# adaLN tiles of a hybrid decoder step in groups, from buffers of their own

## The chip, the cores and the metric

The kernel runs on one core of a Trainium2 chip. The metric is the device time of one execution in microseconds (us): the median of three runs. One further execution was recorded by the profiler; all rows below are from that one. The engines are named as in the profile: PE is TensorE (PEld its weight loads), DVE is VectorE, ACT is ScalarE, POOL is GpSimd, and SP is SyncE, whose queue issues nearly all loads.

## The reference

One step of a decoder trunk of two layers, over 320 token columns: 256 of a prompt and 8 x 8 of eight sample sequences. Layer 0 mixes tokens with a gated MLP over chunks, layer 1 with a Mamba-2 scan; each is followed by an MLP with a squared ReLU. Every sub-layer is preceded by an RMS norm whose shift, scale and gate come from a conditioning vector c for each of nine sequences (adaLN).

```
mod = (silu(c) @ ada_w[i] + ada_b[i]).reshape(c.shape[0], N_MOD, D_MODEL)   # 9 x 6 x 1024, for i in 0, 1
h = modulate(rms_norm(x, norm1_g[i]), mod[:, 0], mod[:, 1])                 # h * (1 + scale) + shift
z = gelu(h @ w_in); u = z[..., :2048]; v = layer_norm(z[..., 2048:], ln_g, ln_b)
y = (u * s) @ w_out            # s: v mixed along the tokens by w_s, plus b_s
x = x + mod[:, 2] * y
x = x + mod[:, 5] * (square(relu(modulate(...) @ w1)) @ w2)
```

The matrix ada_w is read whole, 1024 x 6144 floats for each layer, and multiplies only nine rows.

## The kernel before

**Weights.** All weights are float32 and come in tiles of 128 x 1024 (512 KB). raw_tile takes one of NRAW = 6 slots; split (lines 131 to 136) makes of a tile a rounded part whi (ScalarE, L134) and the rest wlo (VectorE, L135), in NHI = 3 pairs of buffers. A product is three matmuls, hi x hi, lo x hi and hi x lo (mm3: L299 to L301 in the profile). A slot is free again when wlo is made.

**adaLN.** A tile of ada_w is not split. TensorE multiplies it with sc, the silu of c (32 columns), as four instructions of 128 x 256, each into 32 partitions of one PSUM bank (L157). A unit (l, f), f being one of the six parts of layer l, takes eight tiles; then ScalarE copies the sums (L168), four short matmuls turn them (L171) and VectorE adds the bias (L174). Ten units go through ada_unit, a generator that stops after each tile. They are a filler: wload, the loader of weights, takes one step of it for each weight tile (RATE0 = 1.0; RATE1 = 0.7 in the first MLP). need(l, f) runs it until a unit is done. Parts (0, 0) and (0, 1), shift and scale of the first norm, don't go this way.

**First stage.** For kt in 0 to 7 two tiles of ada0 (shift and scale of the 128 features kt) are loaded, multiplied (L429), copied by ScalarE (L439), turned by four short matmuls (L442) and added (L445, L446). With them the features kt of x are normalised into hhi and hlo (L257 to L259; L448 to L455 for the sample columns, also into hs), and a tile of gm_wv0 (the first half of v's weights) is loaded and split. Then 16 matmuls over 512 columns (v_mm: L403 to L407) add these features' part to the first half of v. The loads for kt + 1 are written before the matmuls of kt.

**Second stage.** The second half of v (gm_wv, wload), with adaLN steps between. Then vx, the sample rows, is put together with a copy vs (L471, L472), the layer norm of v runs on VectorE in two halves q (L508 with the row lng, L509 with lnb; these are broadcast loads, one buffer each, in the pool gp that stays open), and 16 projections u (gm_wu) follow, with the mixing matmuls (spatial) from the tenth on. Then come w_out, MLP, the Mamba stage (w_in; there bc and ea, rows spread over all partitions, are loaded through the same queue, L632 and L633), its w_out, and the second MLP.

**Order.** A scheduler orders the instructions by a timeline of its own and places each engine's instructions in a row. Every engine works its row in order; so does SyncE, where a load that waits for a buffer holds all loads behind it. hs and vs lie in a pool g1 that is closed before the norm; a second pool g1, for bsr, wsT and bd, takes its place.

## Time and profile before

| | |
|---|---|
| three runs | 1102.05, 1106.19, 1108.08 us; median 1106.19 |
| the profiled execution | 1104.12 us, its span 1102.3 us |
| TensorE, matmuls | busy 1055.1 us (96%), 7809 records |
| VectorE, ScalarE, POOL | 658.6, 547.1, 315.9 us |
| adaLN of the ten units (L157) | 640 records, 52.9 us busy, mean 390 ns |
| loads by SP's queue | 200.47 MB, 55.5% of the DMA engines' time |

How to read it: TensorE's matmuls overlap, and their ends are modelled, so a busy share says little; the distance from one start to the next is what a matmul costs. One float32 matmul instruction makes two records: a tile of adaLN, four instructions, is a row of "x8". A row of the timeline joins equal instructions that follow each other; in square brackets stands the idle time before it, and what ended it. A row of the busy time by windows has, behind the window and its length, the busy us and (in brackets) the count of PE, PEld, DVE, ACT and POOL, then the granted clock of TensorE as a share of full speed, the DMA share and GB/s.

### The profile page before, as it was taken

Reading aid. Unit: us, or ns where it says so; the run is one execution under the profiler, and the core shown is the slowest. Engines: PE = TensorE matmul, PEld = TensorE weight load, DVE = VectorE, ACT = ScalarE, POOL = GpSimd, SP = SyncE. Lnnn points to the kernel's source line nnn. Section 1 sums busy time; section 2 is a strip of 40 time slices with the busy share of each in tenths; the row PEclk is TensorE's granted clock in tenths of the full one; section 3 lists DMA queues with packets and bytes.
Section 4 is the critical chain, followed back from the end, with each engine's and each line's share of the span. In section 5 each row is a group of like instructions: output and inputs, shape, how many; then the busy total and the mean of one; then the engine's idle time right before and its main releaser. Section 6 shows DMA issues by size and latency. Waiting matters only on the chain.

```text
span 1102.3 us, 19778 instructions
## 1 busy us (share of the span) xinstructions
PE 1055.1 (96%) x7809; PEld 971.5 (88%) x7809; DVE 658.6 (60%) x1080; ACT 547.1 (50%) x1013; POOL 315.9 (29%) x403
## 2 busy tenths in 40 slices
PE   5999999999999999999997989999899999999996
PEld 3677899889899889999996879999899899999996
DVE  3544956445744433445995898988866764443342
ACT  4443333434544433334879666787435455543331
POOL 1200124332333312113361343434325243320111
PEclk9999999999999999999998998999999999999998
DMA  8877885675777767545444555655445565444531
GB/s 330 305 234 231 282 316 186 213 245 177 239 216 219 220 219 222 169 145 194 131 149 152 204 199 191 207 200 203 144 140 183 180 216 167 153 147 143 152 95 48
DMA packets 60877, 213.97 MB, mean 194 GB/s; under 512 B 6560, under 2 KB 12128, under 8 KB 58480
## 3 DMA queue, kind: packets, MB, share of 16 engines
q1 hardware_dynamic: 58544, 200.47, 55.5%
q0 software_dynamic: 1952, 11.98, 3.1%
q8 instruction: 61, 1.00, 0.4%
q14 instruction: 32, 0.26, 0.1%
q10 hardware_dynamic: 288, 0.26, 0.1%
HBM read 199.31 MB, written 12.85 MB: 192 GB/s over the span
## 4 chain that ended last, share of the span: by engine, by line
PE 71%; ACT 8%; DVE 6%; issue 5%; DMA 4%; POOL 3%; POOLq 0%; ACTq 0%; SPq 0%; DVEq 0%
PE mm L299 19%; PE mm L301 18%; PE mm L300 18%; PE adap L157 4%; ACT bc L646 2%; ACT whi L134 2%; DVE wlo L135 2%; DVE co L608 1%; DMA bc<-rowd 1%; PE ax L716 1%; PE mm L403 1%; PE mm L404 1%; PE mm L405 1%; POOL Y L728 1%; PE ax L299 1%
## 5 line engine op out<-in xcount | busy, mean ns | idle before, releaser
L135 DVE TENSOR_TENSOR wlo<-raw,whi 128x1024 fp32r<-128x1024 f32 (+1 forms) x243 | 297.2, 1224 | 225.1 <-ACT whi L134 224.1
L134 ACT ACTIVATE whi<-raw 128x1024 fp32r<-128x1024 f32 (+1 forms) x243 | 254.8, 1050 | 277.2 <-PE mm L300 197.9
L299 PE MATMUL mm<-hhi,whi 128*128 128x320 f32 x952 | 305.4, 321 | 11.1 <-ACT cb L601 5.3
L300 PE MATMUL mm<-hlo,whi 128*128 128x320 f32 x952 | 298.8, 314 | 0.9 <-DVE hlo L831 0.8
L301 PE MATMUL mm<-hhi,wlo 128*128 128x320 f32 x952 | 298.4, 314 | 0.0
L299 PEld LDWEIGHTS mm<-hhi,whi 128*128 128x128 f32 x952 | 182.0, 191 | 29.0 <-issue 13.0
L300 PEld LDWEIGHTS mm<-hlo,whi 128*128 128x128 f32 x952 | 182.5, 192 | 2.0 <-DVE hlo L831 1.1
L301 PEld LDWEIGHTS mm<-hhi,wlo 128*128 128x128 f32 x952 | 182.0, 191 | 0.7 <-issue 0.2
L299 PE MATMUL mm<-mhi,whi 128*128 128x320 f32 x512 | 159.1, 311 | 0.0
L301 PE MATMUL mm<-mhi,wlo 128*128 128x320 f32 x512 | 158.1, 309 | 0.0
L300 PE MATMUL mm<-mlo,whi 128*128 128x320 f32 x512 | 157.9, 308 | 0.0
L350 POOL TENSOR_TENSOR ta<-ta 128x320 f32<-128x320 f32 x64 | 81.5, 1275 | 142.3 <-ACT ta L348 126.8
L299 PEld LDWEIGHTS mm<-mhi,whi 128*128 128x128 f32 x512 | 96.1, 188 | 4.1 <-issue 4.1
L300 PEld LDWEIGHTS mm<-mlo,whi 128*128 128x128 f32 x512 | 96.1, 188 | 0.0
L301 PEld LDWEIGHTS mm<-mhi,wlo 128*128 128x128 f32 x512 | 96.1, 188 | 0.0
L285 POOL TENSOR_TENSOR x<-x,rs 128x64 f32<-128x64 f32 x28 | 12.1, 431 | 222.8 <-DVE rs L284 222.8
L351 ACT ACTIVATE mhi<-ta 128x320 fp32r<-128x320 f32 x64 | 30.1, 470 | 79.1 <-POOL ta L350 79.1
L352 DVE TENSOR_TENSOR mlo<-ta,mhi 128x320 fp32r<-128x320 f32 x64 | 34.7, 548 | 53.7 <-ACT mhi L351 53.7
L608 DVE SCALAR_TENSOR_TENSOR co<-cb,vec,co 128x344 f32<-128x344 f32 x96 | 54.5, 580 | 7.4 <-ACT co L606 7.2
L157 PE MATMUL adap<-raw,sc 128*32 128x256 f32 x640 | 52.9, 390 | 0.2 <-DMA raw<-ada_w 0.2
L602 POOL COPY cvp<-cb 128x3 f32<-128x3 f32 x32 | 24.1, 753 | 70.3 <-ACT cb L600 70.2
L282 DVE SCALAR_TENSOR_TENSOR x<-mm,mod,x 128x256 f32<-128x256 f32 x29 | 14.0, 483 | 46.5 <-PE mm L301 45.2
(340 smaller groups left out, 1752.0 us busy)
## 6 DMA issues: line engine op xcount, KB each, us to landing
raw<-mlp_w SPq DMA_DIRECT2D x128, 512.0 KB, 3.9
raw<-ada_w SPq DMA_DIRECT2D x80, 512.0 KB, 4.4
raw<-w_in SPq DMA_DIRECT2D x48, 512.0 KB, 3.6
raw<-ada SPq DMA_DIRECT2D x16, 512.0 KB, 5.9
raw<-gm_wv SPq DMA_DIRECT2D x16, 512.0 KB, 5.5
raw<-gm_wu SPq DMA_DIRECT2D x16, 512.0 KB, 5.5
raw<-gm_wo SPq DMA_DIRECT2D x16, 512.0 KB, 4.5
st<-state SPq DMA_DIRECT2D x8, 1024.0 KB, 5.5
```

What stands on the lines that cost most here:

```text
L134: act.activation(hi[:, :n], raw[:, :n], AF.Copy)
L135: eng.tensor_tensor(lo[:, :n], raw[:, :n], hi[:, :n].bitcast(F32), SUB)
L157: pe.matmul(ps[32 * j : 32 * j + 32, :256], lhsT=sc[:, k, :], rhs=r[:, j * 256 : (j + 1) * 256], start=(k == 0), stop=(k == KD - 1), skip_ ...
L299: pe.matmul(ps[:, :n], lhsT=whi[:, kk, :], rhs=hi, start=first, stop=False)
L300: pe.matmul(ps[:, :n], lhsT=whi[:, kk, :], rhs=lo, start=False, stop=False)
L301: pe.matmul(ps[:, :n], lhsT=wlo[:, kk, :], rhs=hi, start=False, stop=last)
L350: pool.tensor_tensor(s, t, t, MUL)
L351: act.activation(mhi[:, m, :], s, AF.Copy)
L352: dve.tensor_tensor(mlo[:, m, :], s, mhi[:, m, :].bitcast(F32), SUB)
L602: pool.tensor_copy(cvp[:, ct, :], cb[:, TP : TP + 3])
L608: dve.scalar_tensor_tensor(o[:, :CO], cb[:, k : k + CO], wv(k), o[:, :CO], MUL, ADD)
L646: act.activation(bc[:, h, cq[c]], bc[:, h, cq[c]], AF.Relu, bias=nat[:, c, HG * g_ + h : HG * g_ + h + 1], scale=-1.0)
```

## The change

**First stage.** ada0 and gm_wv0 come from a pool of ten slots of their own (raw0), closed after the stage. The loads go in groups of kt, (0), (1, 2), (3, 4), (5, 6), (7): first the adaLN tiles of a group, then its v tiles. The adaLN products of a group are written together, the last-loaded tile first, ahead of the v matmuls of the group before; each half of the PSUM bank takes one kt.

**Later adaLN tiles.** ada_unit loads four tiles into buffers of their own (ara, AB = 4), one a step, and after the fourth writes all 16 instructions at once, the last-loaded tile first. The number of steps for a unit stays eight.

**Room.** NRAW goes from 6 to 5; lng and lnb go into the second pool g1; the ring of descriptors for POOL's transfers gets 4096 bytes.

**Second stage.** Its instructions are not to be scheduled before the first stage's last load (issue_after).

```diff
-NRAW = 6
+NRAW = 5
+AB = 4
+NRAW0 = 10
...
     def ada_unit(l, f):
         ps = ada_ps()
-        for k in range(KD):
-            r = raw_tile()
-            nc.sync.dma_start(r, io["ada_w"][l, k * P : (k + 1) * P, f * 1024 : (f + 1) * 1024])
-            for j in range(4):
-                pe.matmul(
...
-            if k < KD - 1:
+        for kb in range(0, KD, AB):
+            rs = []
+            for k in range(kb, kb + AB):
+                r = wp.tile([P, 8 * P], F32, tag="ara", name=nm("ara"), bufs=AB)
+                nc.sync.dma_start(r, io["ada_w"][l, k * P : (k + 1) * P, f * 1024 : (f + 1) * 1024])
+                rs.append(r)
+                if len(rs) < AB:
+                    yield True
+            for i in (AB - 1, *range(AB - 1)):
+                for j in range(4):
+                    pe.matmul(
...
+            if kb + AB < KD:
                 yield True
...
+    s0, s0p = new_pool("right")
     def load(src):
-        raw = raw_tile()
-        nc.sync.dma_start(raw, src)
+        raw = s0p.tile([P, 8 * P], F32, tag="raw0", name=nm("raw0"), bufs=NRAW0)
+        aw["last"] = nc.sync.dma_start(raw, src).ins
...
+    kgs = [(0,), (1, 2), (3, 4), (5, 6), (7,)]
+    def ada_load(kg):
+        for kt in kg:
+            aw[kt] = [load(io["ada0"][kt, hf]) for hf in range(2)]
+        for kt in kg:
+            vw[kt] = load(io["gm_wv0"][kt])
+
+    def ada_mm(kg):
+        ps = ada_ps()
+        for kt, hf in [(kt, hf) for kt in reversed(kg) for hf in (1, 0)]:
+            o = 256 * (kt - kg[0])
+            for j in range(4):
+                pe.matmul(
+                    ps[32 * j : 32 * j + 32, o : o + 256],
...
+        for kt in kg:
+            o = 256 * (kt - kg[0])
+            sb = scratch()
+            act.copy(sb[:, :256], ps[:, o : o + 256])
...
+    for kg in kgs[:2]:
+        ada_load(kg)
+    ada_mm(kgs[0])
+    ada_mod(0)
+    ki = 1
+    for kt in range(KD):
+        if kt % 2 == 0 and ki < len(kgs):
+            ada_mm(kgs[ki])
+            ki += 1
+            if ki < len(kgs):
+                ada_load(kgs[ki])
+        elif kt % 2:
+            for k in kgs[ki - 1]:
+                ada_mod(k)
+        whi, wlo = split(vw[kt])
...
+    with tc.issue_after(aw["last"]):
+        for j in range(2, 4):
...
-        gg = gp.tile([P, 1024], F32, tag="lng", name=nm("lng"))
-        be = gp.tile([P, 1024], F32, tag="lnb", name=nm("lnb"))
+        gg = g1.tile([P, 1024], F32, tag="lng", name=nm("lng"))
+        be = g1.tile([P, 1024], F32, tag="lnb", name=nm("lnb"))
...
-    nc = bacc.Bacc("TRN2", target_bir_lowering=False, num_devices=1)
+    nc = bacc.Bacc("TRN2", target_bir_lowering=False, num_devices=1, dynamic_dma_scratch_size=4096)
```

The places in the new order on which the steps rest follow. A number in a name tells one buffer's fill from the next; whi and wlo carry that of their split, and the lines are each kernel's own.

TensorE at the start, before: raw_177 to raw_184 are the adaLN tiles of kt 0 and 1, and L403 is the first v matmul.

```order
L429 MATMUL adap_181<-raw_177,sc 32x256 x4
L202 MATMUL nrm_143<-ones_d,acc_141 128x1 x3
L429 MATMUL adap_181<-raw_179,sc 32x256 x4
L197 MATMUL nrm_154<-nid,nx_147 128x128 x2
L197 MATMUL nrm_154<-nid,nx_147 128x64
L442 MATMUL adap_181<-cst,ta_200 128x10 x2
L429 MATMUL adap_235<-raw_182,sc 32x256 x4
L429 MATMUL adap_235<-raw_184,sc 32x256 x4
L403 MATMUL mm_171<-whi_196,hhi 128x512
```

After, the same place:

```order
L210 MATMUL nrm_143<-ones_d,acc_141 128x1 x3
L446 MATMUL adap_198<-raw_182,sc 32x256 x4
L446 MATMUL adap_198<-raw_180,sc 32x256 x4
L205 MATMUL nrm_154<-nid,nx_147 128x128 x2
L205 MATMUL nrm_154<-nid,nx_147 128x64
L463 MATMUL adap_198<-cst,ta_207 128x10 x2
L446 MATMUL adap_213<-raw_192,sc 32x256 x4
L446 MATMUL adap_213<-raw_190,sc 32x256 x4
L446 MATMUL adap_213<-raw_188,sc 32x256 x4
L446 MATMUL adap_213<-raw_186,sc 32x256 x4
L414 MATMUL ax_173<-whi_246,hs 128x512
```

The four tiles of kt 1 and 2 now stand ahead of the first v matmuls, and raw_192, the one loaded last of them, stands first.

TensorE between two u projections, before: one adaLN tile stands between them.

```order
L300 MATMUL mm_996<-hlo,whi_1005 128x320
L301 MATMUL mm_996<-hhi,wlo_1006 128x320
L157 MATMUL adap_957<-raw_1036,sc 32x256 x4
L299 MATMUL mm_1035<-hhi,whi_1044 128x320
L300 MATMUL mm_1035<-hlo,whi_1044 128x320
L301 MATMUL mm_1035<-hhi,wlo_1045 128x320
```

After:

```order
L308 MATMUL mm_1028<-hlo,whi_1033 128x320
L309 MATMUL mm_1028<-hhi,wlo_1034 128x320
L165 MATMUL adap_958<-ara_1064,sc 32x256 x4
L165 MATMUL adap_958<-ara_959,sc 32x256 x4
L165 MATMUL adap_958<-ara_994,sc 32x256 x4
L165 MATMUL adap_958<-ara_1029,sc 32x256 x4
L307 MATMUL mm_1063<-hhi,whi_1084 128x320
```

Four tiles stand in one run, and no such run stands at most of the other projections. Counted over the whole order, TensorE's 320 instructions of the ten units lie in 78 runs before and in 29 after; 15 of the 29 are whole quads.

SyncE in the u projections, before: raw is a weight tile of gm_wu or an adaLN tile of ada_w.

```order
L145 DMA raw_1198<-gm_wu 128x1024
L155 DMA raw_1231<-ada_w 128x1024
L145 DMA raw_1243<-gm_wu 128x1024
L155 DMA raw_1277<-ada_w 128x1024
L505 DMA lng_944<-ln_g 128x1024
L145 DMA raw_1283<-gm_wu 128x1024
L155 DMA raw_1316<-ada_w 128x1024
L145 DMA raw_1322<-gm_wu 128x1024
L155 DMA raw_1365<-ada_w 128x1024
L145 DMA raw_1371<-gm_wu 128x1024
L155 DMA raw_1414<-ada_w 128x1024
L506 DMA lnb_945<-ln_b 128x1024
```

After, from the first lng on:

```order
L544 DMA lng_935<-ln_g 128x1024
L545 DMA lnb_936<-ln_b 128x1024
L159 DMA ara_1115<-ada_w 128x1024
L159 DMA ara_1150<-ada_w 128x1024
L159 DMA ara_1185<-ada_w 128x1024
L159 DMA ara_1220<-ada_w 128x1024
L147 DMA raw_1315<-gm_wu 128x1024
L147 DMA raw_1360<-gm_wu 128x1024
L544 DMA lng_945<-ln_g 128x1024
L147 DMA raw_1421<-gm_wu 128x1024
L147 DMA raw_1466<-gm_wu 128x1024
L147 DMA raw_1511<-gm_wu 128x1024
```

The second lng load (lng_944, now lng_945) stood behind eight loads of gm_wu and stands behind eleven; the first, which stood among the first loads of the first stage, stands here too.

SyncE in the Mamba stage, before: raw is a tile of w_in, bc the broadcast rows of a group.

```order
L145 DMA raw_7108<-w_in 128x1024
L629 DMA st_5494<-state 128x2048
L145 DMA raw_7189<-w_in 128x1024
L145 DMA raw_7255<-w_in 128x1024
L632 DMA bc_6340<-rowd 128x1280
L633 DMA ea_6341<-rowd 128x4x192
L145 DMA raw_7317<-w_in 128x1024
```

After:

```order
L147 DMA raw_6965<-w_in 128x1024
L668 DMA st_5495<-state 128x2048
L147 DMA raw_7023<-w_in 128x1024
L147 DMA raw_7109<-w_in 128x1024
L147 DMA raw_7190<-w_in 128x1024
L671 DMA bc_6341<-rowd 128x1280
L672 DMA ea_6342<-rowd 128x4x192
L147 DMA raw_7256<-w_in 128x1024
```

The broadcast bc_6340, now bc_6341, has one weight load fewer ahead of it: 32 since the stage's first, where there were 33.

## Rows read from the trace of the kernel before

**Rows 1.** TensorE over a long even stretch: the view of busy time by windows. Columns below.

```profile
240.00:485.00 245.00, 245.00 (x1775) 224.50 (x1774) 115.06 (x162) 105.21 (x172) 65.85 (x68) 1.00 0.66 207
```

**Rows 2.** TensorE's timeline around one adaLN tile: start us, us, engine, line, operation, count.

```profile
112.95 0.30 PE L301 MATMUL mm<-hhi,wlo 128*128 128x320 f32 x1
113.19 0.64 PE L157 MATMUL adap<-raw,sc 128*32 128x256 f32 x8
113.76 0.41 PE L299 MATMUL mm<-hhi,whi 128*128 128x320 f32 x1
114.01 0.31 PE L300 MATMUL mm<-hlo,whi 128*128 128x320 f32 x1
...
114.45 0.31 PE L300 MATMUL mm<-hlo,whi 128*128 128x320 f32 x1
```

**Rows 3.** The same view where two adaLN tiles lie in one run.

```profile
880.21 1.07 PE L157 MATMUL adap<-raw,sc 128*32 128x256 f32 x16
881.21 0.41 PE L299 MATMUL mm<-hhi,whi 128*128 128x320 f32 x1
```

**Rows 4.** The same view at a run of one instruction, two records.

```profile
196.09 0.62 PE L157 MATMUL adap<-raw,sc 128*32 128x256 f32 x2
196.64 0.41 PE L300 MATMUL mm<-ulo,whi 128*128 128x320 f32 x1
```

**Rows 5.** The same view at the start of the first stage.

```profile
17.52 1.93 PE L429 MATMUL adap<-raw,sc 128*32 128x256 f32 x16 [0.56 <-PE adap L442]
19.38 1.65 PE L403 MATMUL mm<-whi,hhi 128*128 128x512 f32 x3
...
22.69 0.85 PE L405 MATMUL mm<-whi,hlo 128*128 128x512 f32 x3
```

**Rows 6.** SyncE's queue at the start: the timeline of its DMA issues.

```profile
3.07 2.37 SPq L419 DMA_DIRECT2D raw<-ada  x4
5.48 0.70 SPq L419 DMA_DIRECT2D raw<-gm_wv  x1
```

**Rows 7.** DMA issues of two short windows: KB each, us from issue to landing.

```profile
raw<-ada SPq DMA_DIRECT2D x1, 512.0 KB, 7.7
raw<-gm_wv SPq DMA_DIRECT2D x1, 512.0 KB, 10.4
```

**Rows 8.** TensorE's waits, 24 to 100 us: us in total, times, longest.

```profile
PE adap L442 <- ACT ta L439: 0.9, 2, 0.5
PE mm L403 <- ACT hhi L258: 0.8, 1, 0.8
```

**Rows 9.** SyncE's waits, 100 to 145 us, same columns.

```profile
SPq L505 <- DVE mv L187: 5.8, 1, 5.8
```

**Rows 10.** Timeline rows of VectorE, SyncE, ScalarE and TensorE around the norm.

```profile
109.74 2.29 DVE L472 TENSOR_TENSOR vx<-vx,vs 64x2048 f32<-64x2048 f32 x1 [2.70 <-DMA vs<-vx]
...
119.17 4.52 DVE L509 SCALAR_TENSOR_TENSOR v<-v,mv,lnb 128x1024 f32<-128x1024 f32 x2
...
125.01 0.33 SPq L505 DMA_DIRECT2D lng<-ln_g  x1
...
129.63 2.48 DVE L508 SCALAR_TENSOR_TENSOR v<-v,mv,lng 128x1024 f32<-128x1024 f32 x2 [0.92 <-DMA lng<-ln_g]
...
135.09 1.06 ACT L134 ACTIVATE whi<-raw 128x1024 fp32r<-128x1024 f32 x1 [2.90 <-DMA raw<-gm_wu]
...
136.78 0.64 PE L171 MATMUL ax<-cst,adas 128*128 128x36 f32 x4 [1.58 <-ACT adas L168]
```

**Rows 11.** Busy time by windows behind that stall, columns as in rows 1.

```profile
137.00:140.00 3.00, 3.00 (x21) 2.54 (x21) 1.41 (x3) 1.38 (x2) 0.00 (x0) 0.74 1.05 381
140.00:143.00 3.00, 3.00 (x22) 2.69 (x20) 1.01 (x2) 0.00 (x0) 0.00 (x0) 0.70 0.90 324
```

**Rows 12.** ScalarE's wait for the broadcast rows, 577 to 800 us.

```profile
ACT bc L646 <- DMA bc<-rowd: 21.5, 5, 7.8
```

**Rows 13.** SyncE's queue in the Mamba stage, timeline of its issues.

```profile
625.99 4.86 SPq L145 DMA_DIRECT2D raw<-w_in  x2
```

## What I predicted, and how

> **What bounds the kernel now.** I read the busy time by stretch first, then TensorE's timeline, then its waits, then SyncE's queue. In the longest even stretch TensorE is busy 245.00 of 245.00 us [rows 1], and the list of its waits is nearly empty; so between the start and the Mamba stage the time is the sum of what TensorE issues, and a term counts in full if it shortens that issue. Waiting is left at three places: the start, until the first adaLN tile lands [rows 6, 7]; a stall of 1.58 us in the u projections, with a low clock behind it [rows 10, 11]; and the Mamba stage, where ScalarE waits for broadcast rows [rows 12].
>
> **The later adaLN tiles, four at a time.** What does one tile cost TensorE? Around a single tile the matmuls over 320 columns start 0.147 us apart (three steps from 114.01 to 114.45); the tile starts 0.24 us after the last of them, the next ordinary matmul starts 0.57 us after the tile, and the one after that 0.25 us later [rows 2]. From 112.95 to 114.01 are 1.06 us where two ordinary steps would take 0.29: a tile alone costs 0.77. With two tiles in one run the next matmul starts 1.00 us after the run's start [rows 3], so the second tile adds 0.43, and 0.34 is paid per run, for going over to 32 columns and back. A run of a single instruction (two records) takes as long as a whole tile: 0.55 us to the next start [rows 4]. So a run costs 0.34 + 0.43 x (instructions / 4, rounded up).
>
> The order gives the runs. Before, the 80 tiles lie in 78 runs, with 85 rounds of up to four instructions; after, in 29 runs with 86 rounds, since the scheduler still breaks some quads. Before: 78 x 0.34 + 85 x 0.43 = 63.1 us. After: 29 x 0.34 + 86 x 0.43 = 46.8. **Saved: 16.2 us**, nearly all of it where TensorE is never idle. That two becomes four at the same 0.43 is an extension of a row; if the fourth cost as much as the first, nothing would be saved, and that is a rival below.
>
> What could take it back is a wait for the tiles. The four buffers come free only when the run before is done, and their loads stand in SyncE's queue, with weight loads behind them. In the new order 6 to 8 more weight tiles have been issued ahead of each such load than TensorE has finished by the run that frees its buffers, and the run that needs the four stands at least 64 instructions later, 64 x 0.147 = 9.4 us. A tile that finds an empty queue lands sooner than the first one here, which took 7.7 us behind x [rows 7]. I take 0; were each of the 20 quads late by 0.5, it would be +10, and both ends stay in the range.
>
> **One weight slot fewer.** Until now the adaLN tiles took turns with the weights in the six slots; now weights have five of their own. Where adaLN tiles run that is more room, and elsewhere a load is issued one tile later, still four tiles (over 10 us) ahead. Value 0. The smaller descriptor ring concerns POOL's own transfers, which are issued singly and far apart; nothing in the trace waits for one of them but the addition of vs, so the value is 0, and I put no bound on it beyond the room of the range.
>
> **The first stage.** Its loads land in the order of issue: the first adaLN tile at 3.07 + 7.7 = 10.8 us, the fifth tile at 5.48 + 10.4 = 15.9 [rows 6, 7], so four tiles take 5.1 and one takes 1.28 us, which for 512 KB is 410 GB/s. After the change TensorE has the four tiles of (1, 2) ahead of its first v matmul, the last of them first. That is tile seven: 10.8 + 6 x 1.28 = 18.5. At the start 16 records (two tiles) take from 17.52 to 19.38 [rows 5], so four take 3.7, until 22.2; behind them on TensorE stands every v matmul, and ScalarE's two copies stand ahead of the first hhi. I put the first hhi matmul at 24.5, 5.1 us later than the 19.38 of before. Against that, more is done by then: another pair of tiles (2 x 0.43 + 0.34 = 1.2), two modulation groups of four short matmuls (0.5 each; four ordinary starts of 0.147 are 0.6), four hs matmuls (4 x 0.23), and the eight first matmuls that took 3.31 us from 19.38 to 22.69, which is the lower clock of 1.2 GHz, where 0.23 each would be 1.8 [rows 5]. 1.2 + 1.0 + 0.9 + 1.5 = 4.6, so the start costs +0.5; if the clock rises later, up to +2. From there on three runs replace five (-0.7), and of the 1.7 us of waits for copies and hhi [rows 8] I leave 0.7, since at each group the hhi still queues behind two copies on ScalarE: -1.0. **Together -1.2**, from -3 to +3.
>
> The Trainium skill (DMA: Bandwidth & Descriptors, section Bandwidth) says that a load from HBM is bound on the HBM side, near 358 GB/s for a core. The 410 GB/s worked out from the landings above [rows 6, 7] disagree; by the page's figure a tile would take 1.46 us, tile seven would land at 19.6, and the start would cost 1.1 us more.
>
> The second stage's loads, now behind the first's last, cost nothing: the first stage's 24 tiles are through after 10.8 + 23 x 1.28 = 40 us and a little for the load of constants between them, and TensorE still has then more than half of the first stage's 128 v matmuls before it. Nor can they compete with the first stage any more, which is why its tiles keep their 1.28.
>
> **The layer norm's rows (lng, lnb).** Today SyncE stands 5.8 us at the second lng load [rows 9], until VectorE gives the buffer back; the gm_wu loads behind it come late, ScalarE's split starts at 135.09 after 2.90 us of waiting for one, the adaLN copy behind it is late, and TensorE stands 1.58 us [rows 10]. Then the clock falls: 0.74 and 0.70 of full in the next two stretches of 3 us, (0.26 + 0.30) x 3 = 1.7 us lost [rows 11]. After the change three gm_wu loads that stood behind the second lng stand ahead of it, and the weights have their own five slots: -3.3. A new wait comes: the first lng, one of the earliest loads before, now lies where vs lay and can't be issued before VectorE's addition ends at 109.74 + 2.29 = 112.0 [rows 10]. An lng load issued at 125.0 was there at 129.6 [rows 10]; three loads stand ahead of the new one (1.1 MB, 2.8 us at 410 GB/s), so it lands near 121 (with 1.5 us of issuing). VectorE has splits and statistics to do until then: in the same place of its order, behind the sixth split, it begins its next norm operation at 119.17 today [rows 10], and has less to do before it after the change; I put it at 118.5. Behind the waiting operation on VectorE is the split of the seventh gm_wu tile, and TensorE waits for that. Bounds 0 and 2.5, with a clock dip 5; I take 1.3. **Together -2.0**, from -3.3 to +2.
>
> **Sum.** 16.2 + 1.2 + 2.0 = 19.4; 1104.12 - 19.4 = 1084.7 for a run like the profiled one. That run lies 2.1 us under the median of the three runs, 1106.19; I forecast **1086**.
>
> **Rivals.** *Half of it comes back.* VectorE in the u projections or the start gives TensorE new waits (the upper ends above: +3, +2, and a part of the +10 for late quads). For it: VectorE has most of its stretch filled at the norm, and four tiles must all have landed where one was enough. Against it: the lead of 6 to 8 weight tiles. It gives 1092 to 1100. *Nothing changes.* If 0.34 belonged to each tile and not to each run, 16.2 would be 0, and the rest -3: about 1103. The run of two tiles [rows 3] speaks against it, but is not one of four; or if the freed time only lets TensorE run into the splits of the weights, which stand two or three tiles ahead. *Slower: the Mamba stage.* There ScalarE waits 21.5 us in five waits for the broadcast rows, and one such load follows on two weight loads whose issue took 4.86 us, since they wait for slots [rows 12, 13]. With five slots the weight load ahead of it would wait for one tile more, 24 x 0.147 = 3.5 us or more of TensorE's time; eight times 3.5 to 6 is 28 to 48, and from 1084.7 + 2 that makes 1115 to 1135. It decides where the number of weight loads ahead of a broadcast stays as it is. The order speaks against it: ahead of the broadcast bc_6340 stand 33 weight loads before and 32 after, so that the last waits for the same tile's slot. *Better than forecast:* operations of VectorE and ScalarE stand in another order in the Mamba stage, and up to a quarter of those 21.5 us (5 us) may go, or come: 1076 to 1080.
>
> **How the numbers follow.** Forecast (1080 to 1092) 0.56; half of it back 0.20; better 0.10; nothing 0.08; slower 0.06. A difference under 0.5%, 5.5 us, can't be told from no change here: faster means under 1100.7, which the first three cases hold, 0.86; same 0.08; slower, over 1111.7, 0.06. The range reaches down into the better case and up through most of the half case: 1075 to 1097.
>
> **What would show it.** Right: the adaLN line in about 29 runs, a whole quad taking 1.86 us to the next matmul; the first u projection some 3 us earlier; no TensorE wait over 1 us before the Mamba stage; the Mamba stage as long as now within 5 us. Wrong: TensorE idle before adaLN runs with a DMA as releaser, the first hhi matmul after 27 us, VectorE standing at the first lng for over 3 us, or broadcast rows that land later against the weights.

## The result, and the profile after

The changed kernel took 1084.94, 1085.64, 1088.30 and 1089.08 us, median 1086.97; the kernel before, beside it, 1104.61 (four runs). The ratio is 0.9837, 95% interval 0.9803 to 0.9871. The profiled execution took 1088.30 us with a span of 1086.5, so 15.8 us less than the profiled one of before.

Where the 15.8 us went, from the starts of matmuls in the two timelines:

| from ... to | before | after | difference |
|---|---|---|---|
| start to the first u projection | 99.89 | 96.26 | -3.63 |
| u projections, gate and gm_wo, to MLP0's first matmul | 155.30 | 148.84 | -6.46 |
| MLP0, to the Mamba stage's first matmul | 254.47 | 247.18 | -7.29 |
| Mamba stage, to MLP1's first matmul | 346.31 | 346.41 | +0.10 |
| MLP1 and end | 246.37 | 247.84 | +1.47 |

Of the last row, 1.1 us are half clock at the end of the kernel (it cost 5.2 us after, 4.1 before).

The time per group of the adaLN line (TensorE; records, busy us and mean ns, idle time ahead of it):

```profile
L165 PE MATMUL adap<-ara,sc 128*32 128x256 f32 x640 | 43.0, 383 | 0.0
```

A whole quad in TensorE's timeline, answering [rows 2, 3]:

```profile
163.64 0.33 PE L558 MATMUL ax<-bd,vx 128*128 128x64 f32 x2
163.90 1.93 PE L165 MATMUL adap<-ara,sc 128*32 128x256 f32 x32
165.76 0.41 PE L307 MATMUL mm<-hhi,whi 128*128 128x320 f32 x1
166.01 0.31 PE L308 MATMUL mm<-hlo,whi 128*128 128x320 f32 x1
```

Four tiles, 32 records, hold TensorE for 1.86 us; four single tiles took 4 x 0.57 and the way in each time [rows 2]. The timeline has 29 such runs where there were 78. No run waits for a tile (idle 0.0). In the busy time by windows of the whole MLP0 TensorE is never idle before, as in [rows 1], and after it waits once, 0.45 us for ScalarE, not for a tile (first row before, second after):

```profile
255.19:509.66 254.47, 254.47 (x1830) 235.61 (x1829) 119.73 (x165) 108.43 (x174) 65.16 (x66) 1.00 0.63 198
245.10:492.28 247.18, 246.73 (x1830) 237.49 (x1829) 118.37 (x166) 109.04 (x174) 65.38 (x66) 1.00 0.61 207
```

The first stage in TensorE's timeline, answering [rows 5]:

```profile
12.08 1.93 PE L446 MATMUL adap<-raw,sc 128*32 128x256 f32 x16
...
17.60 3.64 PE L446 MATMUL adap<-raw,sc 128*32 128x256 f32 x32 [1.35 <-DMA raw<-ada]
21.18 0.61 PE L414 MATMUL ax<-whi,hs 128*128 128x512 f32 x1
...
23.83 0.48 PE L411 MATMUL mm<-whi,hhi 128*128 128x512 f32 x1
24.15 0.40 PE L412 MATMUL mm<-wlo,hhi 128*128 128x512 f32 x1
...
34.05 0.61 PE L463 MATMUL adap<-cst,ta 128*128 128x10 f32 x4 [0.77 <-ACT ta L457]
```

The seventh tile ends the wait at 17.60, the first hhi matmul starts at 23.83, and of the later waits 0.77 is the only one left over half a microsecond [rows 8]. And what is new, around the norm (timeline of VectorE, GpSimd, SyncE and TensorE), where [rows 10] stood:

```profile
105.65 2.29 DVE L511 TENSOR_TENSOR vx<-vx,vs 64x2048 f32<-64x2048 f32 x1 [2.93 <-DMA vs<-vx]
...
109.98 0.57 SPq L544 DMA_DIRECT2D lng<-ln_g  x1
...
112.41 2.01 POOL L524 TENSOR_TENSOR wsT<-wsT,cst 128x1024 f32<-128x1024 f32 x1 [3.89 <-DMA wsT<-gm_wsT]
112.49 3.01 DVE L137 TENSOR_TENSOR wlo<-raw,whi 128x1024 fp32r<-128x1024 f32 x1
...
116.01 2.73 DVE L547 SCALAR_TENSOR_TENSOR v<-v,mv,lng 128x1024 f32<-128x1024 f32 x2
118.84 1.28 DVE L547 SCALAR_TENSOR_TENSOR vx<-vx,mv,lng 64x1024 f32<-64x1024 f32 x1
120.15 1.28 DVE L548 SCALAR_TENSOR_TENSOR v<-v,mv,lnb 128x1024 f32<-128x1024 f32 x1
121.35 1.22 DVE L137 TENSOR_TENSOR wlo<-raw,whi 128x1024 fp32r<-128x1024 f32 x1
122.62 0.41 PE L309 MATMUL mm<-hhi,wlo 128*128 128x320 f32 x1 [2.00 <-DVE wlo L137]
```

TensorE stands 2.00 us for the split of the seventh gm_wu tile, which VectorE reaches only behind the norm's first four operations; the clock is then at half for 3.4 us, as the windows show (columns as in [rows 1], clock 0.83):

```profile
120.00:130.00 10.00, 8.00 (x63) 6.62 (x62) 9.50 (x18) 3.06 (x5) 0.00 (x0) 0.83 0.96 355
```

The old stall of 1.58 us [rows 10, 11] is gone, and this one, 0.4 us longer, is in its place. In the Mamba stage ScalarE's wait for the broadcast rows (us in total, times, longest) reads, against [rows 12]:

```profile
ACT bc L685 <- DMA bc<-rowd: 19.5, 4, 8.5
```

**The clock has to be taken out before stages are compared.** The trace gives the stretches in which TensorE had half its clock (1.2 instead of 2.4 GHz); half of their length is what they cost at most, since a part that falls into a wait of TensorE costs nothing (3.4 us of a stretch in e8, so 1.7 of its 5.1). The start is not in these records: they begin 15.8 to 22.4 us into the trace, and ahead of them the granted clock reads 1.00 while the rows run at half speed (32 records took 3.58 us at 17.60, and 1.86 at 163.90). For the new first stage that matters little: in e9 those 32 records ran at full speed, and the first hhi matmul came only 0.1 us sooner (23.73, 23.83). The table has, for every profiled run, in us: the time to the Mamba stage's first matmul, what the low clock cost in it, the rest; the same for the Mamba stage.

| kernel | to the Mamba stage | low clock | at full clock | Mamba stage | low clock | at full clock |
|---|---|---|---|---|---|---|
| before | 509.7 | 1.7 | 508.0 | 346.3 | 13.7 | 332.7 |
| before, again (e12) | 509.8 | 1.7 | 508.1 | 354.5 | 22.2 | 332.3 |
| changed | 492.3 | 1.7 | 490.6 | 346.4 | 17.1 | 329.3 |
| changed, again (e9) | 493.3 | 3.4 | 489.9 | 347.7 | 17.1 | 330.7 |
| e1, one tile | 506.7 | 3.4 | 503.3 | 345.0 | 13.7 | 331.4 |
| e2, two tiles | 494.4 | 0.0 | 494.4 | 346.5 | 15.4 | 331.2 |
| e3, grouping alone | 500.7 | 3.4 | 497.3 | 350.9 | 22.2 | 328.7 |
| e4, all 16 first | 494.1 | 5.1 | 489.0 | 342.4 | 11.9 | 330.4 |
| e5, no mask product | 498.0 | 5.1 | 492.9 | 349.9 | 20.5 | 329.4 |
| e6, first stage alone | 508.3 | 1.7 | 506.6 | 345.7 | 13.7 | 332.1 |
| e7, unbroken, norm late | 484.9 | 0.0 | 484.9 | 340.6 | 10.2 | 330.4 |
| e8, no queueing | 502.4 | 5.1 | 497.3 | 348.1 | 18.8 | 329.3 |
| e10, copy on ScalarE's queue | 492.7 | 1.7 | 491.0 | 343.1 | 15.4 | 327.7 |
| e11, five slots alone | 509.9 | 0.0 | 509.9 | 342.6 | 13.7 | 329.0 |

At full clock a kernel repeats itself within 0.7 us to the Mamba stage (before 508.0 and 508.1, changed 490.6 and 489.9) and within 1.4 in it; the low clock moves by 8.5 us between two runs of the kernel before. So the change is worth 17.4 to 18.2 us ahead of the Mamba stage. There it has 25 runs and 76 rounds (a round is up to four of these instructions) where the kernel before has 72 and 77; the other four of its 29 runs lie behind it.

### The profile page after: what moved, and what is told of

It reads as the page before. It is cut to its first block, busy times and chain, and to the rows that moved or that the text cites. A ratio compares the mean times of both kernels' runs of the same rounds, so it can differ in the third digit from the quotient of the medians.

```text
span 1086.5 us, 19726 instructions
## 1 busy us (share of the span) xinstructions
PE 1038.2 (96%) x7809; PEld 979.4 (90%) x7809; DVE 656.7 (60%) x1080; ACT 549.1 (51%) x1013; POOL 318.3 (29%) x403
## 4 chain that ended last, share of the span: by engine, by line
PE 76%; ACT 7%; DVE 6%; issue 5%; DMA 4%; POOL 3%; SPq 0%; POOLq 0%; ACTq 0%; DVEq 0%
PE mm L307 20%; PE mm L308 19%; PE mm L309 19%; PE adap L165 3%; ACT bc L685 2%; PE ax L755 2%; DMA bc<-rowd 1%; PE mm L411 1%; DVE wlo L137 1%; PE mm L412 1%; DVE co L647 1%; PE mm L413 1%; ACT whi L136 1%; DMA raw<-ada 1%; POOL Y L767 1%
## 5 line engine op out<-in xcount | busy, mean ns | idle before, releaser
L137 DVE TENSOR_TENSOR wlo<-raw,whi 128x1024 fp32r<-128x1024 f32 (+1 forms) x243 | 300.9, 1239 | 207.8 <-ACT whi L136 207.0
L293 POOL TENSOR_TENSOR x<-x,rs 128x64 f32<-128x64 f32 x28 | 11.1, 397 | 218.7 <-DVE rs L292 218.6
L165 PE MATMUL adap<-ara,sc 128*32 128x256 f32 x640 | 43.0, 383 | 0.0
L307 PE MATMUL mm<-uhi,whi 128*128 128x320 f32 x128 | 40.0, 315 | 0.0
```

The lines of the kernel that those rows point to most:

```text
L137: eng.tensor_tensor(lo[:, :n], raw[:, :n], hi[:, :n].bitcast(F32), SUB)
L165: pe.matmul(ps[32 * j : 32 * j + 32, :256], lhsT=sc[:, kb + i, :], rhs=rs[i][:, j * 256 : (j + 1) * 256], start=(kb + i == AB - 1), stop=( ...
L307: pe.matmul(ps[:, :n], lhsT=whi[:, kk, :], rhs=hi, start=first, stop=False)
```

## The experiments

**Theory:** a run of 32-column matmuls costs TensorE some 0.34 us beside 0.43 per round of four, and 49 runs fewer are the gain. **Rival:** the price belongs to the tile, and the gain is the first stage's or the norm's.

**e1: one tile at a time again.**

```diff
-AB = 4
+AB = 1
...
-                r = wp.tile([P, 8 * P], F32, tag="ara", name=nm("ara"), bufs=AB)
+                r = wp.tile([P, 8 * P], F32, tag="ara", name=nm("ara"), bufs=4)
...
-                        stop=(kb + i == KD - 2),
+                        stop=(kb + i == (KD - 2 if AB > 1 else KD - 1)),
```

> The changed kernel with one thing undone: each adaLN tile again issues its four matmuls as soon as it is there (groups of one; the same four buffers, first stage, slots and norm rows as in the changed kernel). Its order has 79 runs and 87 rounds of 32-column matmuls, the changed kernel 29 and 86. If a run costs 0.34 us and a round 0.43 (the theory), it is 50 x 0.34 + 0.43 = 17.4 us slower than the changed kernel: 1087.0 + 17.4 = 1104.4, which is what the kernel before takes (1104.6). If 0.34 belongs to every tile (the rival), the grouping gave nothing and it stays at 1087 to 1088, a ratio of 0.984 to the kernel before. The stall of 2.0 us at the norm may go or come with the order: 3.7 us either way.

1096.40 us (six runs), ratio 0.9922 (0.9897 to 0.9948). The rival falls: 9.4 us of the gain are lost. It is not the 17.4, for two reasons that the table shows. Here TensorE has no wait at the norm (2.0), and six runs had a mean clock of 0.983, against 0.978 and 0.980 in the changed kernel's. At full clock e1 needs 503.3 - 490.6 = 12.7 us more to the Mamba stage; with the 2.0 of the wait that the changed kernel has and e1 has not, 14.7 for the 48 runs and two rounds that it has more there: some 0.3 per run. The cleanest place is MLP0, where neither kernel has half clock and e1 differs from the changed kernel in nothing else. It takes e1 as long as the kernel before, to 0.01 us, where the changed kernel takes 247.18; so slots, first stage and norm have no part in that difference:

```profile
252.26:506.74 254.48, 254.48 (x1831) 235.62 (x1829) 119.72 (x165) 108.44 (x174) 65.12 (x66) 1.00 0.63 198
```

**e2: two at a time.** As e1, with `AB = 2`.

> The changed kernel with the adaLN tiles in groups of two instead of four, everything else as in it. Its order has 47 runs and 89 rounds. By 0.34 per run and 0.43 per round it takes 18 x 0.34 + 3 x 0.43 = 7.4 us more than the changed kernel: 1094.4, ratio 0.991 to the kernel before. By the rival (a price per tile) 1087 to 1088. A cost that falls only with the fourth tile would show as 1100 or more.

1094.31 us, ratio 0.9889 (0.9857 to 0.9922): the forecast by run and round. At full clock 3.8 us more than the changed kernel to the Mamba stage, 5.8 with the wait of 2.0 that it hasn't; the formula said 7.4, of which 7.1 (17 runs and 3 rounds) lie there. The price falls with the number of runs, not with the fourth tile.

**e3: the grouping alone, in the kernel before.** `ada_unit` as in the changed kernel; first stage, lng and lnb as before.

```diff
-NRAW = 6
+NRAW = 5
+AB = 4
...
-nc = bacc.Bacc("TRN2", target_bir_lowering=False, num_devices=1)
+nc = bacc.Bacc("TRN2", target_bir_lowering=False, num_devices=1, dynamic_dma_scratch_size=4096)
```

> The kernel before with the grouping of four alone and what it needs to fit (five weight slots, the small descriptor ring); the first stage and the place of the norm's rows (lng, lnb prefetched) are as before. 31 adaLN runs and 88 rounds instead of 78 and 85: saved 47 x 0.34 - 3 x 0.43 = 14.7 us. If the terms of the sum are right, the grouping is nearly all of the gain: 1104.6 - 14.7 = 1090, ratio 0.987. If instead the first stage or the norm's rows carried the gain, it stays above 1098.

1100.45 us (twelve runs), ratio 0.9962 (0.9940 to 0.9983): a third of what was expected. In MLP0 it is as fast as the changed kernel (247.18 us); the gain is lost elsewhere. The first u projection begins at 103.13, 3.2 us later than before, 1.7 of it low clock and the rest near what the five slots alone cost (1.3, e11); TensorE stands 2.7 us for a split in the norm's stretch; and the low clock cost 22.2 us in the Mamba stage of the profiled run, with a mean clock of 0.975 over twelve runs against 0.983. To the Mamba stage it gains 10.7 us at full clock; with the 1.3 of the slots and the 1.1 by which its wait is longer than the old stall that is 13 for 45 runs, again some 0.3 per run.

**e4: all 16 matmuls of a quad first.**

```diff
-            for i in (AB - 1, *range(AB - 1)):
+            with tc.high_priority():
+              for i in (AB - 1, *range(AB - 1)):
...
```

> The changed kernel with the 16 matmuls of each quad given the scheduler's highest priority, so that no quad is broken by another matmul: 20 runs and 80 rounds instead of 29 and 86, 9 x 0.34 + 6 x 0.43 = 5.6 us less. In VectorE's order the split of the seventh gm_wu tile now stands ahead of the norm, so the 2.0 us wait behind the norm and the low clock after it (1.7) should go too: 1087.0 - 5.6 - 3.7 = 1077.7, ratio 0.976. Rival: the quads are issued with no slack behind their loads, TensorE then stands for the last tile at each of them (releaser DMA); at 0.5 us for 20 quads that is +10, and the result is 1087 or slower.

1090.82 us, ratio 0.9866 (0.9836 to 0.9895), so no faster than the changed kernel, and at full clock only 1 to 2 us less to the Mamba stage. Of the 7.6 that were expected at full clock, 6.1 lie there (7 runs, 4 rounds and the wait of 2.0). It is the rival, though for two quads and not for all. The scheduler now puts a quad where its loads should have landed, and on the chip two had not (waits of TensorE, 96 to 250 us; total, times, longest):

```profile
PE adap L166 <- DMA ara<-ada_w: 5.9, 2, 3.0
```

The runs themselves are cheaper (the line's busy time is 39.4 us, 43.0 in the changed kernel); the two waits take it back.

**e5: is it GpSimd's product that holds the split up?** The split of the sixth tile takes 3.01 us beside GpSimd's product and ends 1.08 us behind it.

The kernel leaves the mask out, and the spatial matmuls multiply other numbers; the work is otherwise the same.

```diff
-    pool.tensor_tensor(wsT, wsT, mask[:, 0:P].unsqueeze(1).to_broadcast([P, NG, P]), MUL)
```

> The changed kernel without GpSimd's product of wsT with the mask (128x1024, 2.0 us; the unmasked wsT is used, so that the spatial matmuls multiply other numbers); the order of all other work at that place is the same. In the changed kernel VectorE's split of the sixth gm_wu tile took 3.01 us instead of 1.21, starting 0.08 us behind that product and ending 1.08 us after it, four norm operations follow, the seventh split ends at 122.57, and TensorE stood 2.0 us for it, with 3.4 us of half clock behind that. Theory: the product of GpSimd keeps VectorE's split waiting, 1.8 us, and that is what TensorE pays for. Then the wait falls to 0.2 us or less, the low clock at 124 is gone, and the stretch from the first u projection to the first gm_wo matmul... of MLP0's start (148.8 us) is 3.5 us shorter, 145.3. Rival: the four norm operations ahead of the split (5.1 us) are enough; then a wait of 1.5 us or more stays, with the low clock, and nothing is gained.

1086.30 us, ratio 0.9837 (0.9796 to 0.9878): nothing gained, and TensorE's wait at the norm is longer, 4.6 us. VectorE's timeline says why:

```profile
111.54 2.29 DVE L511 TENSOR_TENSOR vx<-vx,vs 64x2048 f32<-64x2048 f32 x1 [6.02 <-DMA vs<-vx]
...
118.38 1.23 DVE L137 TENSOR_TENSOR wlo<-raw,whi 128x1024 fp32r<-128x1024 f32 x1
...
121.95 2.48 DVE L546 SCALAR_TENSOR_TENSOR v<-v,mv,lng 128x1024 f32<-128x1024 f32 x2 [1.86 <-DMA lng<-ln_g]
```

The split is back at 1.23 us, so the product does hold VectorE up; but in this run the copy of vs landed late, VectorE stood 6.02 us at the addition, and the 1.8 us won were spent waiting for lng. My theory of this wait fell. What the runs agree on instead is the addition's time. Each kernel with the changed kernel's order around the norm, in us:

| kernel | copy of vs, issue to landing | addition, behind the first u projection | TensorE's wait |
|---|---|---|---|
| changed | 7.3 | 9.4 | 2.0 |
| changed, again (e9) | 7.4 | 9.5 | 2.0 |
| e10 | 8.1 | 9.9 | 2.9 |
| e8 | 8.8 | 10.9 | 3.5 |
| e5 (without the product) | 10.4 | 12.5 | 4.6 |

VectorE works in order: while it stands at the addition, the splits behind it stand too, and the wait grows nearly one for one with the landing. In e2, with another order of the quads, the copy landed after 4.4 us and there was no wait. These are agreements between profiles; no run moved the landing alone.

**e10: the copy on another queue.**

```diff
-    nc.gpsimd.dma_start(vs_[TS:, :], vx[0:TS, :])
+    nc.scalar.dma_start(vs_[TS:, :], vx[0:TS, :])
```

> The changed kernel with the copy of vs issued on ScalarE's queue instead of GpSimd's; all other work stands in the same order on every engine. In the traces so far the later that copy lands, the longer TensorE stands for the split of the seventh gm_wu tile: landing after 7.3 us, 2.0 us of wait; 8.8 us, 3.5; 10.4 us, 4.6; and none where it landed after 4.4 us. Theory: VectorE stands at the addition of vs until the copy has landed, and what is behind it in VectorE's queue (splits, the first lng load's room, the norm) moves with it, so the copy's landing sets the wait. Off GpSimd's queue it should land in 3 to 5 us; the wait is then gone or under 0.5, with the low clock behind it: 2 to 4 us less in the u projections (148.8 to 145 to 146.5), 1083 to 1085 in all. Rival: the landing is as late on any queue, because the weight loads fill the DMA engines; then nothing changes.

1086.75 us, ratio 0.9833 (0.9800 to 0.9866): nothing gained. The copy's rows (the view of one tile) say that the queue is not what makes it late:

```profile
L510 ACTq DMA_DIRECT2D vs<-vx x1: 515/515/515, 97.5 to 97.5; - x1
...
DMA to landing us min/median/max: 8.1/8.1/8.1
```

The rival holds as far as this goes: landing is no earlier on ScalarE's queue. That the weight loads then in flight (DMA share 0.90 in the window 96 to 120) are the reason was not tried by itself.

**e6: the first stage alone, in the kernel before.** The new first stage with its pool of ten and its queueing; `ada_unit`, six slots, lng and lnb as before.

> The kernel before with the new first stage alone (pool of ten tiles, adaLN part 0 in groups, second stage's loads behind the last of the first); later adaLN tiles singly from six shared slots, norm rows prefetched, as before. By the prediction's term the first u projection starts 1.2 us earlier than before (99.9), at 98.7, and the kernel takes 1103.9; by what the changed kernel's trace leaves when the cheaper adaLN runs are taken off (3.6 - 1.5), 2.2 us earlier, 97.7. Rival: the first stage gains nothing by itself, since TensorE starts its first hhi matmul 4.5 us later; then 100 or more, above all if a low clock falls into the start (half clock for 6.8 us costs 3.4).

The first u projection starts at 97.93, 2.0 us earlier than before (99.89; 100.03 in e12): the second figure of the two, and nearly additive: the changed kernel's 3.6 leave 1.7, and its four adaLN runs fewer in that stretch (4 against 8 in e6) are worth 1.2 to 1.4. The whole took 1100.50 us (twelve runs), ratio 0.9959 (0.9937 to 0.9981), somewhat more than 2 us; the interval reaches from 2.1 to 7.

**e8: without the queueing.**

```diff
-    with tc.issue_after(aw["last"]):
+    if True:
```

> The changed kernel without the rule that queues the second stage's loads behind the last of the first. Nine of them (4.7 MB) then stand in SyncE's queue between the tenth and the fifteenth load of the first stage. At 1.28 us per 512 KB the adaLN tiles of the groups behind them land up to 9 x 1.28 = 11.5 us later. Theory: the first stage is paced by its loads at the second and third group, and the first u projection starts later by 11.5 less the slack of the loads there (some 5 us): 5 to 8 us, at 101 to 104, and the kernel takes 1092 to 1095. Rival: the first stage's loads run far enough ahead of TensorE, and nothing moves (96 to 97).

1097.81 us, ratio 0.9923 (0.9893 to 0.9953), some 10 us slower than the changed kernel (9.5 by the ratios); the first u projection starts at 106.08, 9.8 us later, with a wait of TensorE for the group (3, 4) and half clock in and behind it, which cost 3.4:

```profile
30.54 0.39 PE L415 MATMUL ax<-wlo,hs 128*128 128x512 f32 x1
36.92 3.60 PE L446 MATMUL adap<-raw,sc 128*32 128x256 f32 x32 [5.99 <-DMA raw<-ada]
```

So the queueing is not a detail: without it the new first stage ends 6.2 us later than the old one (99.89).

**e11: five slots and the small ring alone.**

```diff
-NRAW = 6
+NRAW = 5
...
-nc = bacc.Bacc("TRN2", target_bir_lowering=False, num_devices=1)
+nc = bacc.Bacc("TRN2", target_bir_lowering=False, num_devices=1, dynamic_dma_scratch_size=4096)
```

> The kernel before with five weight slots instead of six and the small descriptor ring, nothing else. By the prediction both cost nothing: 1105, same as the kernel before within 3 us. The adaLN tiles still take turns with the weights here, so at most the first stage and the u projections could be tighter: the kernel with grouping alone began its u projections 3.2 us later than the kernel before, 1.7 of it low clock. Rival: the slot costs time in the first stage or in the Mamba stage, 1108 to 1115.

1102.58 us (twelve runs), ratio 0.9972 (0.9953 to 0.9991). The first u projection is 1.3 us later than before (101.29 against 99.89 and 100.03), without a recorded low clock; the Mamba stage takes 329.0 us at full clock, 3.5 less. All eleven profiles with five slots stand at 327.7 to 331.4 there, the three with six slots (two of the kernel before, e6) at 332.1 to 332.7. Operations of that stage stand in another order with five slots; which of them brings it was not tried.

**e9 and e12: both kernels once more.**

> The changed kernel once more, for its own spread and a second profile. Theory: up to the Mamba stage the time at full clock repeats within 2 us (490.6 from the start of the trace to the stage's first matmul), and runs differ by where TensorE's clock falls: 1.7 to 5 us in the start and the u projections, 10 to 20 in the Mamba stage, wherever a wait of 1 to 3 us happens to be followed by half clock. Then the median is 1085 to 1089, runs spread over 1083 to 1096, and a run's time goes against its mean clock. Rival: the changed kernel always loses more to the clock than the kernel before (24 against 19 to 20 us so far, from four runs); then the mean loss stays at 24 or more.

> The kernel before once more, for a second profile. By the theory the time at full clock up to the Mamba stage is again 508 us and in the stage 332 to 333, and only the low clock moves: 10 to 20 us in the stage.

The changed kernel: 1085.25 us (six runs, 1081.95 to 1091.68), ratio 0.9821 (0.9787 to 0.9856); its runs go against their mean clock (correlation -0.93), and the mean clock is 0.9795 after 0.978. The kernel before, one run: 1112.81 us, all but 0.2 us of the excess over the first profile (8.7) in the low clock of the Mamba stage (windows, columns as above; clock 0.95 and 0.94):

```profile
493.32:841.06 347.74, 324.37 (x2708) 311.62 (x2707) 288.57 (x502) 235.19 (x503) 131.96 (x200) 0.95 0.54 177
```

```profile
509.82:864.28 354.46, 330.76 (x2707) 316.98 (x2706) 284.40 (x502) 235.78 (x503) 133.49 (x200) 0.94 0.51 174
```

By the runs' mean clock the changed kernel loses a little more to it than the kernel before (0.978 and 0.9795, against 0.982 to 0.983 over 17 runs each time). That is 3 to 4 us; whether it is a property of its order or chance stays open.

**e7: a version that beats both.** The first matmul of a quad keeps its place, the other 15 follow it at once; and the norm stands behind the split of the seventh gm_wu tile.

`ada4` is one matmul of the quad, `norms` the norm's loads and operations, and `fill["split"]` the last split written.

```diff
...
+            for ij in todo[:1]:
+                ada4(*ij)
+            with tc.high_priority():
+                for ij in todo[1:]:
+                    ada4(*ij)
...
         ev_u(m, proj_h(io["gm_wu"][m]))
+        if m == 6:
+            with tc.issue_after(fill["split"]):
+                norms()
```

> A version meant to beat both. The changed kernel with two additions: the last 15 matmuls of each quad have the scheduler's highest priority (the first one keeps its place), so that there are 20 runs and 80 rounds instead of 29 and 86; and the norm operations stand on VectorE behind the split of the seventh gm_wu tile. By 0.34 per run and 0.43 per round 5.6 us less; the wait of 2.0 us and the low clock after it (1.7) gone: 9.3 us less than the changed kernel, 1077.7, or at full clock 1062.8 - 7.6 = 1055. TensorE should wait for no adaLN tile (the quads start where they did), unlike in the kernel with priority for all 16, which stood twice for 2.9 us. Rivals: the norm, now later, makes the first spatial matmul late by as much; or the clock in the Mamba stage takes back what was gained there, as the last four kernels lost 19 to 27 us to it: then 1082 to 1087.

1079.95 us (six runs, 1073.72 to 1081.05), ratio 0.9758 (0.9729 to 0.9787). TensorE is never idle in the u projections, and no quad waits (busy time by windows; the group of the adaLN line):

```profile
95.46:237.73 142.27, 142.27 (x1144) 133.44 (x1142) 91.24 (x165) 57.68 (x93) 44.66 (x51) 1.00 0.77 270
```

```profile
L164 PE MATMUL adap<-ara,sc 128*32 128x256 f32 x640 | 38.7, 382 | 0.0
```

To the Mamba stage it is 5.7 us faster at full clock than the changed kernel (5.0 by the second profile of that): 2.0 of the wait, and 3 to 3.7 of the runs, where 7 runs and 4 rounds fewer make 4.1 by the formula. VectorE's timeline there, where the split (113.81) now goes ahead of the norm (114.96):

```profile
102.36 2.29 DVE L517 TENSOR_TENSOR vx<-vx,vs 64x2048 f32<-64x2048 f32 x1 [0.87 <-DMA vs<-vx]
...
113.81 1.23 DVE L137 TENSOR_TENSOR wlo<-raw,whi 128x1024 fp32r<-128x1024 f32 x1
114.96 1.28 DVE L554 SCALAR_TENSOR_TENSOR v<-v,mv,lng 128x1024 f32<-128x1024 f32 x1
```

The copy of vs landed after 4.8 us in this run, so e7 alone doesn't tell the new order from an early landing. e4 speaks for the order: there too this split goes ahead of the norm, the copy landed only after 11.1 us, and TensorE waited for no split. It had, however, just stood 2.9 us for a quad (113.65), which gave VectorE time (VectorE in e4):

```profile
113.11 2.29 DVE L512 TENSOR_TENSOR vx<-vx,vs 64x2048 f32<-64x2048 f32 x1 [5.28 <-DMA vs<-vx]
...
123.80 2.25 DVE L137 TENSOR_TENSOR wlo<-raw,whi 128x1024 fp32r<-128x1024 f32 x1 [1.11 <-ACT whi L136]
...
127.07 2.48 DVE L548 SCALAR_TENSOR_TENSOR v<-v,mv,lng 128x1024 f32<-128x1024 f32 x2
```

## Why the prediction was right, and where it was not

**The later adaLN tiles: right, a little large.** 16.2 was the term. The quad takes the 1.86 us that the two-tile run gave, in 29 runs, and no tile is late, so the bound of +10 for late quads had no part in it. e1 puts a run at some 0.3 us instead of 0.34. MLP0, with 31 and 8 runs, 33 and 32 rounds and 0.45 of wait after, at (254.47 - 247.18 + 0.45 - 0.43) / 23 = 0.32: 49 runs are some 15 us. What in going over to 32 columns and back costs it was not tried. The rival "nothing" fell with e1.

**The slot: 0 is not shown.** I put no price on the fifth slot because loads run four tiles ahead. In the old first stage it costs 1.3 us (e11); the changed kernel's first stage has a pool of its own, and no run has that kernel with six slots. In the Mamba stage five slots gained 1 to 5 us at full clock where I had put nothing, or a loss. The ring of descriptors was never varied by itself.

**The first stage: right in kind, larger.** -1.2 was the term, -2.0 came (e6). The seventh tile landed at 17.6, I had 18.5; the first hhi matmul came at 23.83, I had 24.5, so the start cost 4.5 and not 5.1. Four tiles at the low clock take 3.58 us (3.7 was said), and 0.77 of waits is left (0.7). But the path to 24.5, four tiles at the low clock and then ScalarE's copies, isn't what sets the start. In e9 the clock rose earlier and the four tiles took 1.86 us, and yet the first hhi matmul came at 23.73. It stands behind a wait for VectorE's mod, and VectorE is busy from 19.77 with two splits ahead of that (rows of TensorE and VectorE in e9, in order of time):

```profile
17.37 1.93 PE L446 MATMUL adap<-raw,sc 128*32 128x256 f32 x32 [1.30 <-DMA raw<-ada]
19.23 0.50 PE L414 MATMUL ax<-whi,hs 128*128 128x512 f32 x1
19.77 2.37 DVE L137 TENSOR_TENSOR wlo<-raw,whi 128x1024 fp32r<-128x1024 f32 x2 [1.27 <-ACT whi L136]
22.45 0.36 DVE L466 TENSOR_SCALAR mod<-adap,vec 128x9 f32<-128x9 f32 x2
22.86 1.03 PE L463 MATMUL adap<-cst,ta 128*128 128x10 f32 x4 [0.78 <-DVE mod L466]
23.73 0.77 PE L411 MATMUL mm<-whi,hhi 128*128 128x512 f32 x1
```

So that the time came out within 0.7 us was in part luck.

The Trainium skill (DMA: Bandwidth & Descriptors, section Bandwidth) lets the HBM side bind at some 358 GB/s for a core, which by my estimate would have put that tile at 19.6; the same section measures up to 425 GB/s for one core while the other of its pair is idle. This kernel runs on one core, the windows of its start show 413 and 405 GB/s (last column), which agrees with the second figure and not with the first, and the measurement decides:

```profile
8.00:18.00 10.00, 5.91 (x37) 4.39 (x40) 4.72 (x14) 3.35 (x8) 0.78 (x3) 1.00 1.03 413
18.00:40.00 22.00, 20.71 (x138) 15.15 (x131) 12.56 (x29) 10.94 (x25) 5.08 (x12) 1.00 1.02 405
```

That the queued loads cost nothing was right, and e8 shows what they would have cost.

**The norm: the step that failed.** I took -2.0; at full clock nothing was won (a wait of 2.00 us for a stall of 1.58). -3.3 for the old stall and its low clock went as said. For the new wait I took 1.3, from lng landing at 121 against VectorE at 118.5. Instead VectorE was there at 116.01 and lng had landed (4.1 us after its issue at 109.98), yet TensorE stood 2.0 us, and with the low clock 3.7. The mis-sized term is what lies on VectorE ahead of the seventh split: I counted a wait for a load, and did not count the queue that starts with the wait for the copy of vs (2.93 us), holds the addition, a split slowed by GpSimd (3.01) and four norm operations. 3.7 lay inside the bound of 5 that I had given and not taken. The chain by which lng can't be issued before the addition ends is real: VectorE did wait for lng in e5 (1.86 us) and, with the product in place, in e1 (1.76) and e2 (2.29).

**The Mamba stage.** As long as before (346.4 against 346.3), inside the 5 us. ScalarE waits no longer for broadcast rows in total (19.5 us in four waits, 21.5 in five before; the longest 8.5 against 7.8), so the slower rival didn't happen. What the stage won at full clock (2 to 3) the low clock took back in the profiled run.

**The sum.** 15 + 2.0 + 0, and 2 or 3 in the Mamba stage, less what the clock took: 17.6 and 21 us between medians, with 19.4 forecast. The forecast of 1086 (by its own sum 1084.7 + 2.1 = 1086.8) is met (1086.97, 1085.25), by a sum in which the norm was too good and the Mamba stage and the first stage too small, and the half clock took some of it back: that it came within 1 us is luck, the main term is not. Of the signs named, "no TensorE wait over 1 us before the Mamba stage" did not hold, at the norm and, if the first stage is meant too, in the 1.35 us for tile seven; the other signs of being right did.

## To carry to other kernels

In this kernel matmuls over 32 columns between those over 128 are paid by the run, some 0.3 us each, so gather such matmuls, and keep a gathered run whole: let its first instruction wait for its place and the others follow at once. Putting the whole run first makes it wait for its loads (e4). On an engine that works in order, count everything between a wait and the operation that another engine needs, not the wait alone; moving that one operation ahead (e7, with an early landing) left no wait, and removing GpSimd's product from beside that queue (e5) didn't shorten it.

## What the runs showed of the hardware

- Half clock mostly came at or behind waits of TensorE, of 0.5 to 6 us, but not behind all of them, and not only there: in e10 it began at 615.2, with TensorE busy for all 12 us from 603 to 615; behind the same 2.0 us at the norm the clock fell in one run of the changed kernel and not in the other (e9). Ahead of the kernel's end it lasted 3.4, 6.8 or 10.2 us. Between two runs of one kernel that made 8.5 us in the Mamba stage, so differences of a few us between kernels need the clock taken out first.
- GpSimd's product over 128x1024 (2.0 us) makes a split of VectorE (1.23 us alone, e5) last 3.01 where they meet, and in the kernel before, beside two products of GpSimd (118.56 to 122.61), two norm operations lasted 4.52 instead of 2.48 [rows 10]. The Trainium skill says of this pair (SBUF — State Buffer, section SBUF: two separate sides) that they share a port pair as an exclusive lock, also where a VectorE operation has two inputs in SBUF and GpSimd reads SBUF; the trace agrees: the split ended 1.08 us after the product did, not far from the 1.23 that it takes alone.
- A 512 KB copy from SBUF to SBUF landed 4.4 (e2) to 11.1 us (e4) after its issue in these runs, and on ScalarE's queue (8.1) no sooner than on GpSimd's (7.3, 7.4).
